# The opening's splits taken apart and sigmoid pairs set between the heavy ones in a hybrid backbone layer

## The chip, the cores and the metric

The kernel runs on one core of a Trainium2 chip. The metric is the device time of one execution in microseconds (us); lower is better. The engines have short names here as in the profile: PE is TensorE's matmuls and PEld its weight loads, DVE is VectorE, ACT is ScalarE, POOL is GpSimd, SP is the engine that issues most DMA transfers.

## What is computed

One layer with two token mixers side by side: a gated short convolution and an mLSTM that runs over the rows in both directions. Both read one wide input projection.

```python
hx = rmsnorm(x, g_norm) * (1 + scale) + shift          # 2048 x 1024
hc = rmsnorm(ctx, g_norm) * (1 + scale_c) + shift_c    # 256 x 1024
px = hx @ w_in + b_in                                  # 1024 x 11296
u = c_a * x_a
y_a = b_a * conv3(u) * silu(z_a)                       # conv along grid rows of 64
hn = headwise_rmsnorm(mlstm(q, k, v, gates)) * g_head
y_b = sigmoid(o) * hn * silu(z_b)
merged = sigmoid(g_a) * (y_a @ w_pa) + sigmoid(g_b) * (y_b @ w_pb)
out = rmsnorm(x + gate * (merged @ w_out + b_out), g_final)
```

`shift`, `scale` and `gate` come from `silu(c) @ w_ada + b_ada`. All of it is fp32.

## The kernel before

The 2048 rows are worked on in two halves of 1024. The big products keep fp32 accuracy by splitting each operand into a high part, rounded by a cast on ACT, and a low part, the remainder, which DVE gets by subtraction (`split`, L176 to L179); three matmuls, high by high, high by low and low by high, make one product. On top of that stands a scheme with seven block products in place of eight (Strassen and Winograd): a **pair** is a block of 256 output columns (two channel blocks, `i`) by two halves of 512 rows (`j`), and needs the seven left and seven right operands o = 0 to 6. The right ones are made once from the input (`xA`, slots `x`), the left ones from the weights as they stream in (`Stream`: raw weights `wr`, sums `sw`, high and low parts `wh` and `wl`). A pair is 7 x 4 x 3 = 84 matmuls of 128x512 (L415 in `pair`) into PSUM banks X, Y, W, Z, V. As products become ready, DVE adds them up (`u2` at L424, `u3` at L429, `added` at L914), and `fin` finishes the four blocks: one with the third product, the others with the fifth, sixth and seventh. The bank Z gets the seventh product on top of the fifth, so the sum at L914 of the block after the fifth has to be done before.

**The opening** (L1063 to L1241) makes `xA` and works out the first pair, q0, while inputs still land. For each of four column groups kk it has these steps: `ada` (L1092, four quarters n = 0 to 3, 8 matmuls each that the profile shows as 16 records) multiplies w_ada into PSUM tile `pu`, of which there is one; `modulation` (L1099 to L1101) takes shift and scale from there on DVE; `turn_to` (L212) transposes the normed rows on TensorE, four transposes to a block; `modulated` (L216 on ACT, L217 on DVE) applies shift and scale and gives blocks v11, v21, v12, v22; `cut_sums` makes four differences of them (L1136); `cut` splits seven parts; `mms` (L1110) are the matmuls of q0's first four products, `EARLY_OPS`, for this kk. TensorE's row is written out by hand; instructions in `pin` keep the order of the program on their engines, and nearly all of the opening on DVE and ACT is pinned.

**The first half's pairs** come in the order of the string `todo` (L1042). The letters are the column blocks of w_in: q, k, v; X, C, Z, B of the convolution branch; o and z (output gate and its silu gate); a and b (the merge gates g_a and g_b, whose `fin_s` is one tanh on ACT and a store). Of the `fin`s, C has most for DVE (a sum, a product and two shifted taps of the convolution, L982 to L989), z and Z two operations beside the sum, a, b and o none. After v3 the queue `later` runs beside the pairs, one step for each 4.3 matmuls (`run` with 0.235): `prep_b` (norms of the second half's rows, L205, their modulation, differences L295), `late_rows` (gate row L1357, rows of w_out times gate L1380), `ctx_scan` and `state_scan` (state updates: POOL weighs, L641, TensorE multiplies into the one bank `pn`, L646, DVE adds, L648 and L650). The order of the pairs is free as long as X comes before C, C before Z and B, Z before B, and o before z, as these hand tiles on.

Of the kernel before, what the change touches and what calls it, by code (L numbers as in the profile page):

```python
# [10 lines left out]
F32 = mybir.dt.float32  # L11
# [3 lines left out]
OP = mybir.AluOpType  # L15
# [26 lines left out]
def hybrid_kernel(ctx: ExitStack, tc, x, c, ctxt, c_ctx, w_ada, b_ada, g_norm, w_in, b_in,  # L42
                  w_conv, b_conv, g_head, w_pa, w_pb, w_out, b_out, g_final, out):
    nc = tc.nc
# [132 lines left out]
    def split(hi, lo, raw, eng=None, pinned=False):  # L177
        a = nc.scalar.copy(hi, raw)  # L178
        b = (eng or nc.vector).tensor_tensor(lo, raw, hi.bitcast(F32), op=OP.subtract)  # L179
# [123 lines left out]
    class Stream:  # L303
# [16 lines left out]
        def cut(self, raw):  # L320
            hi, lo = self.half()
            split(hi, lo, raw, None, self.pinned)
            return hi, lo

# [717 lines left out]
    todo = plan(kinds, "q0 q1 q2 q3 k0 v0 k1 v1 k2 v2 k3 v3 X0 C0 Z0 B0 X1 C1 Z1 B1 X2 C2 Z2 B2 X3 C3 Z3 B3 "  # L1042
                       "o0 z0 o1 z1 o2 z2 o3 z3 a0 a1 a2 a3 b0 b1 b2 b3")
# [82 lines left out]
    def cut(kk, o, v):
        if kk % 2 == 0:
            xA.claim((o,), (kk // 2,))
        split(xA.at(o, 0, kk), xA.at(o, 1, kk), v, None, True)

    def cut_first(kk):
        cut(kk, 0, vs[kk, 0])
        cut(kk, 2, vs[kk, 1])

    def less(d, a, b):
        pin(nc.vector.tensor_tensor(d, a, b, op=OP.subtract))  # L1136

    def cut_sums(kk):

        v11, v21, v12, v22 = (vs.pop((kk, n)) for n in range(4))  # L1140
        t1, t3 = uslot(), uslot()
        less(t1, v12, v11)
        less(t3, v22, v12)
        cut(kk, 4, t1)
        t2 = v11
        less(t2, v22, t1)
        cut(kk, 3, t3)

        def more():
            t4 = v21  # L1150
            less(t4, v21, t2)
            cut(kk, 1, t2)
            return (kk, 5, t4), (kk, 6, v22)
        return more

    def rest(todo):
        for a in todo:
            cut(*a)
# [17 lines left out]
    normed(4, 5)  # L1176
    modulated(0, (0, 1), None)
    cut_first(0)
    normed(5, 8)
    ada(1, (0,))  # L1180
    turn_to(0, (2, 3), (pa_, pd_))
    modulated(0, (2, 3))
    more = cut_sums(0)
    ada(1, (1,))
    turn_to(1, (0, 1), (pn_, pa_))
    ada(1, (2,))
    turn_to(1, (2, 3), (pa_, pd_))
    ada(1, (3,))
    rest(more())
    modulation(1)  # L1190
    modulated(1, range(4))
    cut_first(1)
    more = cut_sums(1)
    ada(2, (0, 1))
    turn_to(2, (0, 1), (pn_, pa_))
    ada(2, (2, 3))
    turn_to(2, (2, 3), (pa_, pd_))
    modulation(2)
    modulated(2, (0, 1))
# [452 lines left out]
```

## Time and profile before

| | us |
|---|---|
| median of 3 runs | 2679.39 (2679.29 to 2679.91) |
| profiled execution, device time | 2682.87 |
| its span, first to last instruction | 2681.2 |
| first half's pairs from X0 to B3, 383.4 to 714.4 us: TensorE busy / DVE busy | 319.8 / 271.5 |
| first half's pairs from o0 to b3, 714.4 to 1055 us: TensorE busy / DVE busy | 333.5 / 221.6 |

A row of the timeline holds start, duration, engine, line, operation, tiles (out<-in), shape, and in brackets the idle time ahead of it and what ended that. A row of the groups holds the count, then busy time and mean ns of one, then idle time ahead of them and what ended it. Buffer numbers are left out of the names: `x` stands for all slots of operands.

Where TensorE waits from 785 to 1055 us (in total, times, longest):

```profile
PE pn L646 <- DVE tk L650: 2.8, 2, 2.6
PE pn L646 <- DVE cst L648: 2.5, 2, 2.3
PE pn L646 <- POOL vw L641: 0.9, 1, 0.9
```

### The profile page before, as it was taken

The numbers are of one execution on the slowest core, as the hardware profiler recorded it, in microseconds if no ns is written. First come the engines' busy times: TensorE is split into PE (matmuls) and PEld (weight loads), VectorE is DVE, ScalarE is ACT, GpSimd is POOL, SyncE is SP. The second block draws the span as 40 slices with busy tenths as digits, with TensorE's granted clock in tenths as the row PEclk, the third lists the DMA queues.
The fourth block names the chain that finished last, engine by engine and source line by source line (L and its number), as shares of the span: only waits on it lengthen the run. The fifth ranks groups of instructions, "written<-read, shape, count | busy, mean of one in ns | idle before, by whom it ended". The sixth has DMA issues, their size and how long they took to land. (4 is left out here: it accounts for less than half of the span.)

```text
span 2681.2 us, 38175 instructions
## 1 busy us (share of the span) xinstructions
PE 2605.7 (97%) x12807; PEld 2172.1 (81%) x12807; DVE 1728.4 (64%) x3119; ACT 1098.8 (41%) x2269; POOL 1116.0 (42%) x1322
## 2 busy tenths in 40 slices
PE   7999999999999999999999999999999999999998
PEld 6788887887778887877887888888888888888777
DVE  5743238887976657477578667667766656554597
ACT  5433344333443335343443444344444544442333
POOL 1221223233345443235555565565655224422664
PEclk9999999999999999999999999999999999999999
DMA  8323353454643657425653654654466968868542
GB/s 229 96 93 108 102 150 119 157 181 138 228 141 101 179 171 241 127 86 151 193 159 117 198 169 127 181 164 138 151 194 192 307 213 268 256 200 275 200 162 95
DMA packets 373218, 452.99 MB, mean 169 GB/s; under 512 B 24429, under 2 KB 273949, under 8 KB 373021
## 3 DMA queue, kind: packets, MB, share of 16 engines
q1 hardware_dynamic: 372784, 450.46, 54.8%
q8 instruction: 102, 1.67, 0.3%
q14 instruction: 96, 0.78, 0.1%
q10 hardware_dynamic: 236, 0.08, 0.0%
HBM read 319.42 MB, written 131.03 MB: 168 GB/s over the span
## 5 line engine op out<-in xcount | busy, mean ns | idle before, releaser
L415 PE MATMUL pd<-x,wh 128*128 128x512 f32 x5320 | 1699.3, 398 | 22.1 <-DVE t2k L914 12.3
L415 PEld LDWEIGHTS pd<-x,wh 128*128 128x128 f32 x5320 | 986.9, 189 | 218.5 <-issue 25.2
L415 PE MATMUL pd<-x,wl 128*128 128x512 f32 x2660 | 1058.8, 398 | 0.0
L415 PEld LDWEIGHTS pd<-x,wl 128*128 128x128 f32 x2660 | 502.4, 189 | 99.3 <-issue 0.2
L178 ACT CAST wh<-sw 128x512 fp32r<-128x512 f32 x384 | 238.0, 620 | 513.7 <-PE pd L415 422.1
L179 DVE TENSOR_TENSOR wl<-sw,wh 128x512 fp32r<-128x512 f32 x384 | 311.9, 814 | 181.8 <-ACT wh L178 175.2
L178 ACT CAST wh<-wr 128x512 fp32r<-128x512 f32 x352 | 217.5, 618 | 372.1 <-PE pd L415 265.1
L348 POOL TENSOR_TENSOR sw<-wr,sw 128x512 f32<-128x512 f32 x95 | 135.6, 1427 | 446.1 <-DVE wl L179 389.8
L179 DVE TENSOR_TENSOR wl<-wr,wh 128x512 fp32r<-128x512 f32 x352 | 289.9, 824 | 37.9 <-ACT wh L178 36.8
L462 PE MATMUL pd<-x,wh 128*128 128x512 f32 x896 | 281.7, 396 | 0.0
L348 POOL TENSOR_TENSOR sw<-wr 128x512 f32<-128x512 f32 x95 | 130.0, 1369 | 239.6 <-DVE wl L179 233.7
L641 POOL TENSOR_SCALAR vw<-tk,wk 128x129 f32<-128x129 f32 x205 | 154.8, 759 | 125.8 <-PE pn L646 116.7
L462 PEld LDWEIGHTS pd<-x,wh 128*128 128x128 f32 x896 | 166.3, 188 | 32.0
L462 PE MATMUL pd<-x,wl 128*128 128x512 f32 x448 | 173.3, 397 | 0.0
L186 POOL TENSOR_SCALAR ssq<-ssq 128x1 f32<-128x1 f32 x128 | 37.3, 291 | 294.2 <-ACT hf L894 290.4
L914 DVE TENSOR_TENSOR t2k<-pd,u 128x512 f32<-128x512 f32 x168 | 115.5, 688 | 61.7 <-PE pd L415 60.6
L348 POOL TENSOR_TENSOR sw<-sw,wr 128x512 f32<-128x512 f32 x94 | 133.4, 1420 | 48.8 <-DVE wl L179 37.8
L892 ACT ACTIVATE hf<-pn,rd 128x128 f32<-128x128 f32 x128 | 47.0, 368 | 247.0 <-DVE rd L888 226.4
L348 POOL TENSOR_TENSOR sw<-wr,wr 128x512 f32<-128x512 f32 x94 | 132.9, 1414 | 18.7 <-DMA wr<-in_w_in_dram 9.4
L808 POOL TENSOR_SCALAR_AFFINE_SELECT mw<-mw 128x256 f32<-128x256 f32 x128 | 63.0, 512 | 120.9 <-DMA mw<-mwd 89.7
L879 PE MATMUL pn<-tk,pt 128*128 128x129 f32 x512 | 99.2, 276 | 4.7 <-DVE hb L893 4.7
L921 DVE SCALAR_TENSOR_TENSOR t2k<-pd,cols,u 128x512 f32<-128x512 f32 x73 | 54.8, 750 | 73.2 <-PE pd L415 68.3
(255 smaller groups left out, 3349.4 us busy)
## 6 DMA issues: line engine op xcount, KB each, us to landing
wr<-in_w_in_dram SPq DMA_DIRECT2D x176, 512.0 KB, 4.0
tk<-tokd SPq DMA_DIRECT2D x64, 386.0 KB, 3.7
mw<-mwd SPq DMA_DIRECT2D x44, 512.0 KB, 5.0
qkd<-t2k SPq DMA_DIRECT2D x64, 256.0 KB, 3.0
qk<-qkd SPq DMA_DIRECT2D x64, 256.0 KB, 4.0
tk<-tokd SPq DMA_DIRECT2D x48, 257.0 KB, 2.9
tokd<-t2k SPq DMA_DIRECT2D x32, 258.0 KB, 3.2
x<-in_w_ada_dram SPq DMA_DIRECT2D x16, 512.0 KB, 6.2
```

The source lines that it names most:

```text
L178: a = nc.scalar.copy(hi, raw)
L179: b = (eng or nc.vector).tensor_tensor(lo, raw, hi.bitcast(F32), op=OP.subtract)
L186: nc.gpsimd.tensor_scalar(dst, ss, 1.0 / n, EPS, op0=OP.mult, op1=OP.add)
L348: nc.gpsimd.tensor_tensor(s, a, b, op=op)
L415: nc.tensor.matmul(ps[b], op[wi][:, kk, :], xs.at(o, xi, kk), start=(fresh and kk + pi == 0), stop=(o == last[b] and kk == 3 and pi == 2), ...
L462: nc.tensor.matmul(pss[j], ops[k // 4][wi][:, k % 4, :], y(xi, k, j), start=(k + pi == 0), stop=(k == NK - 1 and pi == 2))
L641: pin(nc.gpsimd.tensor_scalar(vw, tk[:, VT], wk, None, op0=OP.mult))
L808: pin(nc.gpsimd.affine_select(mws[m][:, :, 0, d, :], mws[m][:, :, 0, d, :], pattern=[[0, 2], [s, P]], base=0, channel_multiplier=-s, compa ...
L879: nc.tensor.matmul(pn[:, d, :], pt[:, d, :], tk[:, VT], start=True, stop=False)
L892: nc.scalar.activation(hf, pn[:, 0, 0:P], AF.Copy, scale=rd[:, 0:1])
L914: nc.vector.tensor_tensor(t, ps, add, op=OP.add)
L921: nc.vector.scalar_tensor_tensor(dst, ps, bcol(col), add, op0=OP.add, op1=OP.add)
```

## The change

It has two parts. The order of the first half's pairs is another: o and z, and most of a and b, stand between the pairs of the convolution branch. And the opening is written in another order: `split` is taken apart into `high` (casts on ACT) and `low` (remainders on DVE), which are called apart; the four differences come in a row (`less`); the stream of weights holds its remainders back (`held`, `settle`); the last shift and scale (`ada(3)`, `modulation(3)`) comes ahead of the matmuls of q0; and the right operands 5 and 6 of the groups 2 and 3, which only the sixth and seventh product need, come after the first four products. What each engine computes in all is the same.

```diff
+            self.held = None
...
         def cut(self, raw):
             hi, lo = self.half()
-            split(hi, lo, raw, None, self.pinned)
+            if self.held is None:
+                split(hi, lo, raw, None, self.pinned)
+            else:
+                pin(nc.scalar.copy(hi, raw))
+                self.held.append((lo, raw, hi))
             return hi, lo
+
+        def settle(self):
+
+            for lo, raw, hi in self.held:
+                pin(nc.vector.tensor_tensor(lo, raw, hi.bitcast(F32), op=OP.subtract))
+            self.held = []
...
-    todo = plan(kinds, "q0 q1 q2 q3 k0 v0 k1 v1 k2 v2 k3 v3 X0 C0 Z0 B0 X1 C1 Z1 B1 X2 C2 Z2 B2 X3 C3 Z3 B3 "
-                       "o0 z0 o1 z1 o2 z2 o3 z3 a0 a1 a2 a3 b0 b1 b2 b3")
+    todo = plan(kinds, "q0 q1 q2 q3 k0 v0 k1 v1 k2 v2 k3 v3 X0 C0 a0 Z0 b0 B0 o0 z0 X1 C1 a1 Z1 b1 B1 o1 z1 "
+                       "X2 C2 a2 Z2 B2 o2 z2 X3 C3 a3 Z3 B3 o3 z3 b2 b3")
...
+    def high(kk, *parts):
+        for o, v in parts:
+            if kk % 2 == 0:
+                xA.claim((o,), (kk // 2,))
+            pin(nc.scalar.copy(xA.at(o, 0, kk), v))
+
+    def low(kk, *parts):
+        for o, v in parts:
+            pin(nc.vector.tensor_tensor(xA.at(o, 1, kk), v, xA.at(o, 0, kk).bitcast(F32), op=OP.subtract))
+
+    def blocks(kk):
+
+        return (0, vs[kk, 0]), (2, vs[kk, 1])
+
+    def less(kk):
 
         v11, v21, v12, v22 = (vs.pop((kk, n)) for n in range(4))
         t1, t3 = uslot(), uslot()
-        less(t1, v12, v11)
-        less(t3, v22, v12)
-        cut(kk, 4, t1)
-        t2 = v11
-        less(t2, v22, t1)
-        cut(kk, 3, t3)
...
+        for d, a, b in ((t1, v12, v11), (t3, v22, v12), (v11, v22, t1), (v21, v21, v11)):
+            pin(nc.vector.tensor_tensor(d, a, b, op=OP.subtract))
+        return (3, t3), (1, v11), (4, t1), (5, v21), (6, v22)
...
-    normed(4, 5)
+    normed(4, 6)
     modulated(0, (0, 1), None)
-    cut_first(0)
-    normed(5, 8)
-    ada(1, (0,))
+    normed(6, 8)
+    high(0, *blocks(0))
+    low(0, *blocks(0))
+    ada(1, (0, 1))
     turn_to(0, (2, 3), (pa_, pd_))
     modulated(0, (2, 3))
-    more = cut_sums(0)
-    ada(1, (1,))
+    ada(1, (2,))
     turn_to(1, (0, 1), (pn_, pa_))
-    ada(1, (2,))
+    parts = less(0)
+    high(0, *parts)
+    low(0, *parts[:2])
+    ada(1, (3,))
     turn_to(1, (2, 3), (pa_, pd_))
-    ada(1, (3,))
-    rest(more())
     modulation(1)
+    low(0, *parts[2:])
     modulated(1, range(4))
-    cut_first(1)
-    more = cut_sums(1)
     ada(2, (0, 1))
     turn_to(2, (0, 1), (pn_, pa_))
+    high(1, *blocks(1))
+    low(1, *blocks(1))
+    st.held = []
+    st.fill(2)
+    parts = less(1)
+    high(1, *parts)
     ada(2, (2, 3))
     turn_to(2, (2, 3), (pa_, pd_))
     modulation(2)
-    modulated(2, (0, 1))
-    rest(more())
-    modulated(2, (2, 3))
-    st.fill(2)
-    cut_first(2)
+    low(1, *parts)
+    modulated(2, range(4))
+    high(2, *blocks(2))
+    ada(3, (0, 1))
     turn_to(3, (0, 1), (pn_, pa_))
-    ada(3, (0,))
+    ada(3, (2,))
     turn_to(3, (2,), (pa_,))
-    ada(3, (1,))
+    ada(3, (3,))
+    st.settle()
     st.fill(4)
+    low(2, *blocks(2))
+    st.settle()
+    st.held = None
     ops.update((o, st.take(0)) for o in (0, 2, 1, 3))
     ps.update((b, dense_ps()) for _, b in EARLY_OPS)
-    mms(0, (0, 1))
-    more = cut_sums(2)
-    ada(3, (2, 3))
+    mms(0)
     modulation(3)
-    modulated(3, range(3))
-    mms(0, (2, 3))
+    modulated(3, (0, 1))
+    parts = less(2)
+    high(2, *parts[:2])
+    modulated(3, (2,))
     turn_to(3, (3,), (pn_,))
-    rest(more())
-    cut_first(3)
     modulated(3, (3,))
+    low(2, *parts[:2])
+    high(3, *blocks(3))
+    low(3, *blocks(3))
     mms(1)
     mms(2)
-    more = cut_sums(3)
-    rest(more())
+    high(2, parts[2])
+    low(2, parts[2])
+    late = less(3)
+    high(3, *late[:3])
+    low(3, *late[:3])
     mms(3)
     s1, u2, u3 = uslot(), uslot(), uslot()
-    nc.scalar.copy(s1, ps["X"])
+    pin(nc.scalar.copy(s1, ps["X"]))
     ops[4] = st.take(0)
-    fin(0, 0, ps["U"], s1)
+    for i in (3, 4):
+        for kk, part in ((2, parts[i]), (3, late[i])):
+            high(kk, part)
+            low(kk, part)
+        if i == 3:
+            fin(0, 0, ps["U"], s1)
     nc.vector.tensor_tensor(u2, ps["Y"], s1, op=OP.add)
     nc.vector.tensor_tensor(u3, ps["W"], u2, op=OP.add)
```

The first place to see is DVE around the last shift and scale of the opening (`gsc` and `shift` from `pu`). Before, remainders and differences of group 2 (`u`, `cv`, `t2k` and the operands `x`) stand ahead of it:

```order
L346 TENSOR_TENSOR sw_570<-wr_193 128x512
L179 TENSOR_TENSOR wl_573<-sw_570,wh_572 128x512
L1136 TENSOR_TENSOR u_586<-t2k_508,cv_497 128x512
L1136 TENSOR_TENSOR u_587<-t2k_510,t2k_508 128x512
L179 TENSOR_TENSOR x_120_591<-u_586,x_119_590 128x512
L1136 TENSOR_TENSOR cv_497<-t2k_510,u_586 128x512
L179 TENSOR_TENSOR x_122_596<-u_587,x_121_595 128x512
L1099 SCALAR_TENSOR_TENSOR gsc<-pu_538,cols_117 128x2x2
L1100 TENSOR_TENSOR shift<-pu_538,cols_117 128x2x2
L1101 TENSOR_TENSOR gsc<-gsc,cols_116 128x2x2
```

With the change it stands behind the weights' sums and remainders, and the four differences follow it in a row:

```order
L358 TENSOR_TENSOR sw_583<-wr_193 128x512
L1146 TENSOR_TENSOR x_98_519<-cv_510,x_97_518 128x512
L1146 TENSOR_TENSOR x_100_522<-cv_512,x_99_521 128x512
L334 TENSOR_TENSOR wl_581<-sw_578,wh_580 128x512
L334 TENSOR_TENSOR wl_586<-sw_583,wh_585 128x512
L1111 SCALAR_TENSOR_TENSOR gsc<-pu_524,cols_117 128x2x2
L1112 TENSOR_TENSOR shift<-pu_524,cols_117 128x2x2
L1113 TENSOR_TENSOR gsc<-gsc,cols_116 128x2x2
L1157 TENSOR_TENSOR u_615<-t2k_514,cv_510 128x512
L1157 TENSOR_TENSOR u_616<-t2k_516,t2k_514 128x512
L1157 TENSOR_TENSOR cv_510<-t2k_516,u_615 128x512
L1157 TENSOR_TENSOR cv_512<-cv_512,cv_510 128x512
```

Group 2's differences went from ahead of the last shift to behind it.

The second place is DVE at the end of the opening, from the remainder of the fifth product's weight (`wl` from `sw`, bank Z) to that of the sixth (`wl` from `wr`, bank V). Before:

```order
L921 SCALAR_TENSOR_TENSOR t2k_716<-pd_577,cols_116,u_706 128x512
L179 TENSOR_TENSOR x_130_641<-cv_620,x_129_640 128x512
L179 TENSOR_TENSOR x_132_645<-t2k_652,x_131_644 128x512
L179 TENSOR_TENSOR wl_713<-sw_562,wh_712 128x512
L1230 TENSOR_TENSOR u_707<-pd_579,u_706 128x512
L1231 TENSOR_TENSOR u_708<-pd_578,u_707 128x512
L179 TENSOR_TENSOR wl_722<-wr_195,wh_721 128x512
```

With the change:

```order
L179 TENSOR_TENSOR wl_701<-sw_576,wh_700 128x512
L1146 TENSOR_TENSOR x_139_705<-cv_512,x_138_704 128x512
L1146 TENSOR_TENSOR x_139_705<-cv_613,x_138_704 128x512
L933 SCALAR_TENSOR_TENSOR t2k_710<-pd_593,cols_116,u_694 128x512
L1146 TENSOR_TENSOR x_142_714<-t2k_516,x_141_713 128x512
L1146 TENSOR_TENSOR x_142_714<-t2k_634,x_141_713 128x512
L1248 TENSOR_TENSOR u_695<-pd_595,u_694 128x512
L1249 TENSOR_TENSOR u_696<-pd_594,u_695 128x512
L179 TENSOR_TENSOR wl_722<-wr_195,wh_721 128x512
```

The remainders of the operands 5 and 6 and the first block's end came between the two.

The third place is DVE in the eleventh pair of `later`'s stretch, which is Z2 before and a1 now, both behind a C pair. `acc` belongs to the gate row of `late_rows`, `u` are u2 and u3, the last row is the sum of the block after the fifth product. Before:

```order
L424 TENSOR_TENSOR u_5389<-pd_5373,u_5365 128x512
L179 TENSOR_TENSOR wl_5392<-wr_5194,wh_5391 128x512
L179 TENSOR_TENSOR wl_5416<-sw_5413,wh_5415 128x512
L1002 SCALAR_TENSOR_TENSOR t2k_5409<-t2k_5407,t2k_5409 128x512
L1357 SCALAR_TENSOR_TENSOR acc<-xb_5333,sc,acc 128x1024
L1003 TENSOR_TENSOR cv_5235<-cv_5235,t2k_5409 128x512
L429 TENSOR_TENSOR u_5435<-pd_5419,u_5389 128x512
L179 TENSOR_TENSOR wl_5438<-wr_5290,wh_5437 128x512
L914 TENSOR_TENSOR t2k_5454<-pd_5441,u_5435 128x512
```

With the change:

```order
L436 TENSOR_TENSOR u_5389<-pd_5373,u_5365 128x512
L179 TENSOR_TENSOR wl_5392<-wr_5194,wh_5391 128x512
L179 TENSOR_TENSOR wl_5413<-sw_5410,wh_5412 128x512
L1375 SCALAR_TENSOR_TENSOR acc<-xb_5333,sc,acc 128x1024
L441 TENSOR_TENSOR u_5432<-pd_5416,u_5389 128x512
L179 TENSOR_TENSOR wl_5435<-wr_5290,wh_5434 128x512
L926 TENSOR_TENSOR t2k_5451<-pd_5438,u_5432 128x512
```

Z's two operations are gone from between; the rest keeps its order. In the fourth pair (B0 before, Z0 now) the last of the four norms (L205) stands just ahead of such a sum, before and now.

More of the change, by code (lines that the diff above doesn't have):

```diff
@@ L1124, in modulated @@
             pin(modulate(v, pts.pop((kk, n)), kk + 4 * (n % 2), 0, eng))
[L1126 to L1138, printed above, removed]
+    def high(kk, *parts):
[9 more added lines that the diff above has]
+    def less(kk):
         v11, v21, v12, v22 = (vs.pop((kk, n)) for n in range(4))
         t1, t3 = uslot(), uslot()
-        less(t1, v12, v11)
-        less(t3, v22, v12)
-        cut(kk, 4, t1)
-        t2 = v11
-        less(t2, v22, t1)
-        cut(kk, 3, t3)
[L1149 to L1158, printed above, removed]
+        for d, a, b in ((t1, v12, v11), (t3, v22, v12), (v11, v22, t1), (v21, v21, v11)):
+            pin(nc.vector.tensor_tensor(d, a, b, op=OP.subtract))
+        return (3, t3), (1, v11), (4, t1), (5, v21), (6, v22)
     EARLY_OPS = ((0, "X"), (2, "U"), (3, "W"), (1, "Y"))
```

## The prediction

> **What bounds the kernel now.** I read the page first, then TensorE's timeline of the first 95 us, then who TensorE waited for in each stage.
>
> ```profile
> PE 2605.7 (97%) x12807; PEld 2172.1 (81%) x12807; DVE 1728.4 (64%) x3119; ACT 1098.8 (41%) x2269; POOL 1116.0 (42%) x1322
> ```
>
> TensorE is busy for 2605.7 of the span's 2681.2 us. The change leaves the matmuls as they are, so all it can win is the 75.5 us of TensorE's idle time and the stretches in which matmuls run at half the granted clock. Three pieces of the opening on TensorE (start, duration, idle before it and what ended that):
>
> ```profile
> 23.62 3.75 PE L1092 MATMUL pu<-sc,x 128*128 128x128 f32 x16 [2.86 <-DMA x<-in_w_ada_dram]
> ...
> 41.14 0.60 PE L212 MATMUL pt<-ident,xr 128*128 128x128 f32 x4
> ...
> 42.01 3.74 PE L1092 MATMUL pu<-sc,x 128*128 128x128 f32 x32
> 45.59 0.60 PE L212 MATMUL pa<-ident,xr 128*128 128x128 f32 x4
> ...
> 62.69 1.05 PE L212 MATMUL pt<-ident,xr 128*128 128x128 f32 x4 [3.13 <-ACT cv L216]
> ...
> 69.59 0.62 PE L1110 MATMUL pd<-x,wh 128*128 128x512 f32 x2
> ...
> 70.27 0.62 PE L1110 MATMUL pd<-x,wh 128*128 128x512 f32 x2
> ...
> 76.01 0.50 PE L1110 MATMUL pd<-x,wl 128*128 128x512 f32 x1 [1.27 <-DVE wl L179]
> ...
> 85.49 0.62 PE L415 MATMUL pd<-x,wh 128*128 128x512 f32 x2
> ```
>
> The opening ends at 85.49, where the first L415 matmul of the ordinary pairs starts. Two waits stand out, 3.13 and 1.27 us. VectorE in the stretch between the third shift and scale and the last weight remainder shows why:
>
> ```profile
> 45.78 0.16 DVE L1099 SCALAR_TENSOR_TENSOR gsc<-pu,cols 128x4 f32<-128x4 f32 x1 [0.37 <-PE pu L1092]
> ...
> 61.41 0.16 DVE L1099 SCALAR_TENSOR_TENSOR gsc<-pu,cols 128x4 f32<-128x4 f32 x1
> ...
> 82.29 0.69 DVE L179 TENSOR_TENSOR wl<-sw,wh 128x512 fp32r<-128x512 f32 x1 [0.74 <-ACT wh L178]
> ```
>
> ```profile
> L179 DVE TENSOR_TENSOR x<-cv,x 128x512 fp32r<-128x512 f32 x10 | 6.5, 686 | 5.0 <-ACT x L178 5.0
> ...
> L179 DVE TENSOR_TENSOR wl<-sw,wh 128x512 fp32r<-128x512 f32 x4 | 2.8, 691 | 2.1 <-ACT wh L178 2.1
> L921 DVE SCALAR_TENSOR_TENSOR t2k<-pd,cols,u 128x512 f32<-128x512 f32 x3 | 2.2, 748 | 2.3 <-PE pd L1110 2.3
> ...
> L179 DVE TENSOR_TENSOR wl<-wr,wh 128x512 fp32r<-128x512 f32 x3 | 2.0, 686 | 1.0 <-ACT wh L178 1.0
> ```
>
> The second fence groups VectorE's work from 45 to 83 us (busy, mean ns, idle before). 5.0 + 2.1 + 2.3 + 1.0 = 10.4 us of these 38 are waits, mostly because each remainder (lo) is queued straight behind the ScalarE cast (hi) it needs. The last shift and scale (61.41) stands in that row, so TensorE got its last transposes late.
>
> In the first half's heavy pairs TensorE's waits end mostly on VectorE's sums (t2k):
>
> ```profile
> 465.25 0.90 PE L415 MATMUL pd<-x,wh 128*128 128x512 f32 x2 [2.04 <-DVE t2k L914]
> ...
> 529.84 0.70 PE L415 MATMUL pd<-x,wh 128*128 128x512 f32 x2 [1.76 <-DVE t2k L914]
> ...
> 609.38 1.19 PE L415 MATMUL pd<-x,wh 128*128 128x512 f32 x2 [2.73 <-DVE t2k L914]
> ...
> 692.54 0.70 PE L415 MATMUL pd<-x,wh 128*128 128x512 f32 x2 [3.53 <-DVE t2k L914]
> ```
>
> By the sequence of pairs these lie in B0, Z1, Z2 and Z3. The clock stands in the windows view (us; busy of PE, PEld, DVE, ACT, POOL; granted clock; DMA share, GB/s):
>
> ```profile
> 62.80:66.20 3.40, 3.40 (x11) 2.83 (x12) 1.69 (x3) 3.40 (x7) 0.00 (x0) 0.50 0.02 5
> 76.50:79.90 3.40, 3.40 (x10) 2.62 (x9) 1.35 (x3) 0.00 (x0) 0.00 (x0) 0.50 0.00 0
> 608.90:612.30 3.40, 2.92 (x7) 2.38 (x8) 3.40 (x6) 1.99 (x4) 0.00 (x0) 0.51 0.52 154
> 530.40:533.80 3.40, 3.40 (x17) 2.81 (x16) 3.05 (x6) 2.49 (x5) 0.00 (x0) 1.00 0.83 254
> 694.20:697.70 3.50, 3.50 (x17) 2.87 (x16) 3.50 (x6) 2.08 (x4) 0.00 (x0) 1.00 0.81 267
> ```
>
> About 3.4 us at 0.50 follow the waits of 3.13, 1.27 and 2.73 us, none follow those of 1.76 and 3.53. One such stretch costs 1.7 us of TensorE work, where it comes.
>
> **The opening, step by step.** Distances from row to row: two groups of four transposes 0.87 (41.14 to 42.01); one quarter of the shift and scale (16 records) 3.58 / 2 = 1.79 (42.01 to 45.59); three matmuls 0.68 (69.59 to 70.27). Twelve of these are 2.72. A VectorE operation of 512 columns lasts 0.686 and the next starts after about 0.60, as its end is overlapped. On ScalarE:
>
> ```profile
> 38.95 0.78 ACT L216 ACTIVATE t2k<-pa,shift,gsc 128x512 f32<-128x512 f32 x1
> 39.62 0.78 ACT L216 ACTIVATE t2k<-pd,shift,gsc 128x512 f32<-128x512 f32 x1
> ...
> 50.47 1.14 ACT L178 CAST wh<-wr 128x512 fp32r<-128x512 f32 x2
> 51.50 1.15 ACT L178 CAST x<-cv 128x512 fp32r<-128x512 f32 x2
> ```
>
> so 0.67 from one modulation to the next and 0.52 from cast to cast. I laid the new order of the three engines along these distances:
>
> - Up to 23.62 nothing moves on TensorE, since that row waits for a load. The two quarters ahead of the transposes run at half speed as now, to about 29.6; all rows are normed by 25.7.
> - From there TensorE has six double transposes (5.2), ten quarters (17.9), two single transposes (0.9) and seven times twelve matmuls (19.1): 43.1 us, which would end at 72.7.
> - The second shift and scale is 0.87 + 1.79 + 0.87 + 1.79 behind 29.6, the third 8.9 and the fourth 9.3 behind the one before; with some 0.2 for the way to VectorE they fall at 35.2, 44.1 and 53.6 (45.78 and 61.41 now for the last two). The last loads are issued by 42.25 and need about 6.2, so they land by 48.5, ahead of the 51.6 at which TensorE wants them.
>
> ```profile
> 34.73 7.52 SPq L1061 DMA_DIRECT2D x<-in_w_ada_dram x4
> x<-in_w_ada_dram SPq DMA_DIRECT2D x16, 512.0 KB, 6.2
> ```
>
> - VectorE from 44.1: 42 operations at 0.60 and 0.8 for the small ones, 26 us, and 1.9 us of waits that are left (for the last shift, the casts and sw): its last weight remainder starts at 72.2 (82.29 now).
> - One wait is added. Between the remainders of the fifth and the sixth weight (wl of Z and V) stand seven operations, two now; counted the same way the sixth ends at 70.2, and TensorE wants it at 68.0. Behind it in TensorE's row wait the rest of V, the seventh product and q1, so its 2.3 us count in full (with 0.1 for Z's remainder 2.4).
>
> The first L415 matmul comes at 72.7 + 2.4 = 75.1, with 0.2 for the ways between engines at 75.3: **10.2 us earlier**. VectorE gives the same: 82.29 - 72.2 = 10.1. The ScalarE and VectorE operations are the same in number, so nothing is added. The differences in a row cost nothing by themselves, as VectorE is waiting for the third shift (42.6 to 44.1) when they are done. If the 2.3 us wait were followed by a half-speed stretch, 1.7 would come back: 8.5. From below I take 7 (VectorE 10% slower in its 28 us), from above 11.5 (10.4 of waits and the rest of the clock).
>
> **The pairs.** Per pair the later work (norms, differences, rows of w_out, states) is drawn by the number of matmuls, so it stays at its place and the pairs are exchanged under it. Their weight loads and stores go with them, the same in number; the DMA shares of 0.52 to 0.83 above leave them room. At Z1's place stands o0 behind B0, at Z3's place o1 behind B1: the conv work of C, which runs over into the next pair, is gone from there, so 1.76 and 3.53 go. At Z2's place stands a1, but still behind a C. VectorE there:
>
> ```profile
> 603.92 0.68 DVE L1002 SCALAR_TENSOR_TENSOR t2k<-t2k,t2k 128x512 f32<-128x512 f32 x1
> ...
> 606.75 0.68 DVE L1003 TENSOR_TENSOR cv<-cv,t2k 128x512 f32<-128x512 f32 x1
> ...
> 608.55 0.68 DVE L914 TENSOR_TENSOR t2k<-pd,u 128x512 f32<-128x512 f32 x1
> ```
>
> Only the first two leave the row ahead of the sum that TensorE waits for: 2 x 0.60 = 1.2 of the 2.73, and 1.5 stays. That is less than the 1.76 which no slow stretch followed, so I take its 1.7 too (0 if not). The 2.04 us at B0's place stays: the sum waits behind a norm,
>
> ```profile
> 463.14 0.75 DVE L205 TENSOR_SCALAR xb<-xb,rs 128x1024 f32<-128x1024 f32 x1 [1.87 <-POOL rs L187]
> ```
>
> which the new row keeps ahead of the sum. Z0's short waits,
>
> ```profile
> PE pa L1323 <- DVE t2k L217: 1.1, 2, 0.9
> ```
>
> in all 1.1, give 0.5. C2 with a2 now lies beside differences like those that Z1 had: 1.76 - 1.2, +0.5. C3, Z3, B3 now lie beside the state updates, through one PSUM bank (pn):
>
> ```profile
> L646 PE MATMUL pn<-vw,tk 128*128 128x129 f32 x192 | 38.0, 279 | 7.1 <-DVE cst L648 3.2 <-DVE tk L650 2.8 <-POOL vw L641 0.9
> PE pn L646 <- DVE tm L650: 1.4, 3, 0.6
> PE pn L646 <- DVE tk L650: 1.2, 2, 0.7
> ```
>
> Beside o, z, a, b these 192 records waited 7.1 us (first row, 714 to 1055 us); in the second half, where X C Z B lie beside the same updates, the waits for VectorE are 2.6 us in 720 us (the other two). So I add 1.5, between 0 and 7.1. Sum: -1.76 - 3.53 - 1.2 - 1.7 - 0.5 + 0.5 + 1.5 = **-6.7 us**, from -15 (all four waits and both slow stretches gone) to 0.
>
> Nothing else is edited, and the stages behind keep their rows. The profiled execution took 2682.87 us (span and 1.7 around it), 3.5 above the median 2679.39. The terms are differences, so they go onto the median: 2679.4 - 10.2 - 6.7 = **2662.5**.
>
> On the clock, the Trainium skill ("TensorE: Matmul & The Clock Gate", section "Why this matters for your kernels") says to leave no idle gap over some 3 us between bursts, or the clock falls to half. This trace differs: 2.73 was followed by 0.51, 3.53 by 1.00. By that rule the 1.7 at Z2's place would not be won: 2664.2.
>
> **Rivals.**
> - *The opening alone pays* (0.17): C's overrun goes into a as it went into Z, and the states take back what o0 and o1 give: 2679.4 - 10.2 = 2669. For it: the same conv rows stand ahead of a1's sum. Against it: Z1's and Z3's places have no C ahead.
> - *All waits on sums go* (0.14): VectorE catches up in every light pair and the norm no longer binds: -15 in place of -6.7: 2654.
> - *The opening doesn't do what it says* (0.07): its loads or VectorE's row, busy for 26 of 28 us, set the same end, and the pairs alone pay: 2673.
> - *Slower* (0.06): the state updates. There are 96 (two records each), where they are dense one to two or three steps of the later queue, a step to 4.3 matmuls of 0.23, or about 2.5 us. Each needs VectorE to empty pn, and in C each of the last three blocks brings four operations, 2.7 us with their 0.686, to the remainders that are there anyway, within the 2.72 of twelve matmuls. From the point where VectorE is over 2.5 us behind, every update stalls TensorE, with slow stretches behind it. Some 70 of the 96 updates at 0.35 us are 24 us: 2679.4 - 16.9 + 24 = 2686. Against it stand the 2.6 us above.
>
> **How the numbers follow.** My forecast has 0.56, with 2657 to 2668 as its own range. 2654 to 2671 takes in the first two rivals and leaves out some 0.2. A measurement of this kernel tells apart about 0.2% (5.4 us): faster than 2674 are the forecast, the first two rivals and half of the third, 0.90; within it 0.05; slower 0.05.
>
> **What would show it.** First L415 matmul at 75 (73 to 78), last shift and scale on VectorE near 53.6, TensorE without a wait from 30 to 67 us, then one of about 2 us for wl. No wait for t2k near 515 and 675 (Z1's and Z3's old places, moved), one of 1 to 2 us in a1, one of 2 us with the norms of the first group behind a0. Waits of L646 below 9 us up to the half's end. I would be wrong if VectorE's row in the opening has waits of over 4 us after 44, or if L646's waits double.

## The result and the profile after

The changed kernel took **2661.77 us** (median of four runs) against 2679.34 before: ratio 0.9935, 95% interval 0.9924 to 0.9947, 17.6 us faster. A later set of five runs gave 2661.48 (0.9934, 0.9921 to 0.9948). Its profiled execution took 2660.47 us with a span of 2658.7; the one before had 2682.87 and 2681.2. The profiled pair is thus 22.4 us apart, more than the medians, and the difference has to be explained too.

First line of the changed kernel's page (busy us, share of the span, instructions):

```profile
PE 2594.5 (98%) x12807; PEld 2166.7 (81%) x12807; DVE 1722.6 (65%) x3119; ACT 1099.0 (41%) x2269; POOL 1123.8 (42%) x1322
```

TensorE (PE) has the same 12807 matmuls. It is busy for 11.2 us less. Fewer stretches at half speed explain at most 6.6 us of that (they cost 22.3 us of the profile before and 15.7 of this one); what the rest is stays open.

The opening's end on TensorE in the changed kernel (start, duration, idle before it and what ended that), then the last shift and scale and the last weight remainders on VectorE (DVE):

```profile
68.11 0.61 PE L1122 MATMUL pd<-x,wh 128*128 128x512 f32 x2
70.70 0.50 PE L1122 MATMUL pd<-x,wl 128*128 128x512 f32 x1 [1.97 <-DVE wl L179]
...
75.85 0.62 PE L427 MATMUL pd<-x,wh 128*128 128x512 f32 x2
```

```profile
54.00 0.16 DVE L1111 SCALAR_TENSOR_TENSOR gsc<-pu,cols 128x4 f32<-128x4 f32 x1 [0.42 <-PE pu L1104]
...
69.97 0.68 DVE L179 TENSOR_TENSOR wl<-wr,wh 128x512 fp32r<-128x512 f32 x1
...
72.65 0.69 DVE L179 TENSOR_TENSOR wl<-sw,wh 128x512 fp32r<-128x512 f32 x1 [0.74 <-ACT wh L178]
```

The first ordinary matmul (L427, L415 before) stands at 75.85 (85.49 before), the last shift and scale at 54.00 (61.41 before). The one wait that is left behind 30 us is that for the sixth weight's remainder, 1.97 us.

TensorE's main waits in the 32 pairs of the first half, changed kernel:

```profile
456.10 0.54 PE L427 MATMUL pd<-x,wh 128*128 128x512 f32 x1 [2.65 <-DVE t2k L926]
596.35 0.47 PE L427 MATMUL pd<-x,wh 128*128 128x512 f32 x1 [1.03 <-DVE t2k L926]
751.72 0.47 PE L427 MATMUL pd<-x,wh 128*128 128x512 f32 x1 [0.96 <-DVE t2k L926]
783.02 0.35 PE L658 MATMUL pn<-vw,tk 128*128 128x129 f32 x1 [2.33 <-DVE cst L660]
888.17 0.35 PE L658 MATMUL pn<-vw,tk 128*128 128x129 f32 x1 [0.95 <-DVE tk L662]
895.14 0.35 PE L658 MATMUL pn<-vw,tk 128*128 128x129 f32 x1 [1.46 <-DVE tk L662]
1033.10 0.45 PE L658 MATMUL pn<-vw,tk 128*128 128x129 f32 x1 [2.96 <-DVE tk L662]
```

The waits of 1.76 and 3.53 us at Z1 and Z3 have no successor. That of 2.73 became 1.03 in a1; that behind the norms (2.04 in B0) stands in Z0 as 2.65. New are 0.96 in a2, behind C2, and 0.95 and 1.46 in a3, behind C3; the last two stand at matmuls of the state updates (L658, L646 before). The 2.33 and 2.96 were there before, as 2.31 and 2.60.

The same windows view for both kernels: the opening, the pairs q, k and v, the 16 pairs from X0, the next 16, and all behind (us; busy of PE, PEld, DVE, ACT, POOL; granted clock; DMA share, GB/s). Changed kernel, then the one before:

```profile
0.00:75.85 75.85, 62.13 (x408) 56.57 (x408) 49.31 (x94) 40.66 (x69) 11.94 (x28) 0.93 0.77 220
75.85:373.60 297.75, 295.51 (x1582) 249.10 (x1580) 116.54 (x213) 112.33 (x217) 64.59 (x76) 1.00 0.34 105
373.60:696.20 322.60, 317.75 (x1419) 260.52 (x1418) 239.75 (x314) 133.45 (x226) 106.32 (x88) 0.99 0.55 179
696.20:1042.30 346.10, 335.09 (x1538) 275.04 (x1537) 250.54 (x411) 132.70 (x204) 166.53 (x160) 0.99 0.51 153
1042.30:2658.70 1616.40, 1584.03 (x7867) 1325.45 (x7865) 1066.43 (x2089) 679.88 (x1554) 774.40 (x970) 1.00 0.58 182
```

```profile
0.00:85.49 85.49, 67.21 (x408) 58.62 (x408) 50.18 (x94) 41.07 (x69) 10.99 (x28) 0.92 0.68 195
...
383.40:714.40 331.00, 319.80 (x1419) 261.36 (x1418) 271.49 (x349) 124.25 (x214) 107.81 (x88) 0.99 0.52 165
714.40:1055.00 340.60, 333.51 (x1537) 274.04 (x1536) 221.61 (x375) 138.87 (x214) 156.22 (x160) 0.99 0.54 164
1055.00:2681.20 1626.20, 1589.49 (x7867) 1329.03 (x7866) 1068.40 (x2090) 682.41 (x1556) 776.35 (x970) 0.99 0.59 181
```

By stage: opening -9.6, first 16 pairs -8.4, next 16 pairs **+5.5**, and **-9.8** in the stages behind, whose code is the same. Of the 5.5 the forecast had 2.0, of the -9.8 nothing. The experiments ask whether the -9.8 belongs to the change, what gives the 5.5 back, and which part of the opening pays.

### The profile page after: what moved, and what is told of

Its sections match the earlier page's. It is cut to its first block, busy times and chain, and to the rows that moved or that the text cites. A ratio compares the mean times of both kernels' runs of the same rounds, so it can differ in the third digit from the quotient of the medians.

```text
span 2658.7 us, 38177 instructions
## 1 busy us (share of the span) xinstructions
PE 2594.5 (98%) x12807; PEld 2166.7 (81%) x12807; DVE 1722.6 (65%) x3119; ACT 1099.0 (41%) x2269; POOL 1123.8 (42%) x1322
## 4 chain that ended last, share of the span: by engine, by line
PE 48%; DVE 3%; DMA 2%; issue 1%; POOL 1%; ACT 0%; SPq 0%; DVEq 0%; POOLq 0%; ACTq 0%
PE pd L427 29%; PE pd L474 11%; PE pn L891 2%; PE pn L892 2%; PE pa L834 1%; PE pu L658 1%; DMA mgd<-t2k 1%; DVE wl L179 1%; PE pa L849 1%; PE pn L658 0%; PE pa L669 0%; DVE xt L1596 0%; DVE xt L1605 0%; DMA x<-wod 0%; DVE cv L999 0%
## 5 line engine op out<-in xcount | busy, mean ns | idle before, releaser
L427 PE MATMUL pd<-x,wh 128*128 128x512 f32 x5320 | 1695.9, 397 | 15.9 <-DVE xt L1605 8.5
L427 PEld LDWEIGHTS pd<-x,wh 128*128 128x128 f32 x5320 | 985.1, 189 | 209.9 <-issue 19.4
L427 PE MATMUL pd<-x,wl 128*128 128x512 f32 x2660 | 1057.3, 397 | 0.0
L427 PEld LDWEIGHTS pd<-x,wl 128*128 128x128 f32 x2660 | 501.8, 189 | 99.3 <-issue 0.2
L179 DVE TENSOR_TENSOR wl<-sw,wh 128x512 fp32r<-128x512 f32 x382 | 303.2, 795 | 182.0 <-ACT wh L178 177.1
L653 POOL TENSOR_SCALAR vw<-tk,wk 128x129 f32<-128x129 f32 x205 | 161.9, 794 | 120.2 <-PE pn L658 109.7
L891 PEld LDWEIGHTS pn<-tk,pt 128*128 128x128 f32 x512 | 86.8, 190 | 16.2 <-issue 5.8
```

The lines of the kernel that those rows point to most:

```text
L427: nc.tensor.matmul(ps[b], op[wi][:, kk, :], xs.at(o, xi, kk), start=(fresh and kk + pi == 0), stop=(o == last[b] and kk == 3 and pi == 2), ...
L653: pin(nc.gpsimd.tensor_scalar(vw, tk[:, VT], wk, None, op0=OP.mult))
L891: nc.tensor.matmul(pn[:, d, :], pt[:, d, :], tk[:, VT], start=True, stop=False)
```

## What the clock records show, and how lengths are compared

Half-speed stretches make two executions of one kernel differ, so they are dealt with first. In the 14 profiles of this case (the two above and twelve below) every half-speed stretch begins a whole number of steps of 3.413 us after every other of the same execution, to 0.02 us: a raster that runs by itself. Two waits of the kernel before, in windows laid on this raster (same columns):

```profile
605.50:608.91 3.41, 1.14 (x6) 0.60 (x4) 3.41 (x5) 0.00 (x0) 0.24 (x1) 1.00 0.26 92
608.91:612.33 3.42, 2.95 (x7) 2.40 (x8) 3.42 (x6) 2.02 (x4) 0.00 (x0) 0.50 0.52 153
687.44:690.85 3.41, 1.57 (x7) 0.95 (x6) 3.41 (x5) 0.00 (x0) 0.33 (x1) 1.00 1.02 378
690.85:694.27 3.42, 1.73 (x8) 1.45 (x9) 3.07 (x5) 1.81 (x3) 0.00 (x0) 1.00 0.83 255
694.27:697.68 3.41, 3.41 (x17) 2.81 (x16) 3.41 (x6) 2.01 (x4) 0.00 (x0) 1.00 0.80 264
```

The wait of 2.73 us falls into one step, which keeps 1.14 us of TensorE work, and the next step runs at 0.50. The longer wait of 3.53 us is cut by a boundary into two steps with 1.57 and 1.73 us of work, and no step is slow. That is why 2.73 cost a slow stretch and 3.53 none, which the prediction could only note. Over the steps between 90 and 2480 us of all 14 profiles that are not slow themselves: with 1.0 to 1.8 us of idle time 113 steps, none followed by a slow one; with 1.8 to 1.94 us 3 of 10; with 1.95 us or more 33 of 33. Outside these bounds (from 10 us on) idle time alone does not decide: of 35 steps with 1.0 to 1.8 us three were followed by a slow one, with 1.49, 1.70 and 1.76 us. The first of them holds the wait of 1.27 us in the opening of the kernel before:

```profile
73.00:76.50 3.50, 2.01 (x7) 1.13 (x8) 3.50 (x6) 1.33 (x3) 0.00 (x0) 0.99 0.22 75
```

What else counts there stays open. The Trainium skill ("TensorE: Matmul & The Clock Gate", "Why this matters for your kernels") puts the limit at gaps of some 3 us; here a wait of 2.04 was followed by a slow step, and the measurement decides.

So a stage's length at full speed is its length less half of its half-speed time, and a run's is its span times its mean granted clock. Both are used below; the rest of the span is the clock's loss. This is an estimate: a slow step in which TensorE also waits costs less than half of its length, and the runs' granted clocks are on record to 0.001, which is up to 1.3 us of one run. In the four sets of runs that the kernel before has beside the experiments, on three chips, its mean at full speed is 2654.5 to 2654.8 us, so runs of different sets are compared at full speed.

## Experiments

**The two halves of the change by themselves, and the change again** (one chip, five runs each).

The opening alone, the sequence of pairs as before:

```diff
-"... X0 C0 a0 Z0 b0 B0 o0 z0 X1 C1 a1 Z1 b1 B1 o1 z1 X2 C2 a2 Z2 B2 o2 z2 X3 C3 a3 Z3 B3 o3 z3 b2 b3"
+"... X0 C0 Z0 B0 X1 C1 Z1 B1 X2 C2 Z2 B2 X3 C3 Z3 B3 o0 z0 o1 z1 o2 z2 o3 z3 a0 a1 a2 a3 b0 b1 b2 b3"
```

> The opening of the change with the old sequence of pairs. Theory (two independent gains, the opening's about -9.6 us and the pairs' about -3 in their stage): the first L427 matmul at 75.8, the pairs' stage as before shifted by -9.6, median about 2669.5 us against 2679 before. Rival (the -9.8 us that the changed kernel won in stages behind the pairs belongs to the opening, by another phase of everything behind it): -18 to -20 us, about 2660. Rival (that -9.8 is luck of single executions): -9.6 with later stages within 2 us of the old ones.

The pairs alone: the kernel before with the upper one of these two strings.

> The old opening with the new sequence of pairs. Theory: the old opening's end (85.5) stays; the first 16 pairs win about 8 us, the last 16 give back about 5, in all -3 in the stage: about 2676 us. Rival (the gain of -9.8 behind the stage belongs to the sequence of pairs, since it moves what the later queue holds when the stage ends): -11 to -14, about 2666. Rival (order of pairs is worth the predicted -6.7 and the run seen was unlucky): about 2672.5.

The changed kernel, unedited:

> The changed kernel once more, to be compared with its parts on one chip. If the parts add: its gain is the sum of those of the opening alone and the pairs alone within 2 us, about -17.5. If the gain behind the stage needs both or is chance, the sum of the two differs from it by over 3 us, or its later stages differ between the two profiles by over 3 us.

| kernel | median us | ratio, interval | at full speed, mean us | lost to the clock, mean us |
|---|---|---|---|---|
| before (9 runs) | 2678.24 | | 2654.6 | 22.0 |
| opening alone | 2666.13 | 0.9954, 0.9941 to 0.9966 | 2648.2 | 16.0 |
| pairs alone | 2667.91 | 0.9962, 0.9949 to 0.9974 | 2650.9 | 15.5 |
| both | 2661.48 | 0.9934, 0.9921 to 0.9948 | 2644.3 | 14.9 |

At full speed the parts add: -6.4 and -3.7 against -10.3 together. What the clock takes does not add: -6.0 and -6.5 against -7.1, each with a standard error of 1.2 to 1.8 us. By the medians each part alone gave more than its theory (-12.1 for -9.6, -10.3 for -3), and the pairs came nearer to their rival; but what is over is clock, not work. The gap is 5.4 us with a standard error of 2.1; why the clock's share does not add stays open.

**The kernel before once more**, unedited, for a second profile.

> The kernel before once more, for a second profile. Theory (TensorE's idle stretches belong to the order of the work and come back; what varies from run to run is where the half-speed stretches fall, since they start on a raster of 3.413 us that runs by itself, after a raster step in which TensorE was idle for over about 1.95 us): the waits of 2.04, 2.73, 3.53, 2.31, 2.60, 2.59 us (near 465, 609, 692, 800, 1047, 1068) within 0.7 us of these, all half-speed starts a multiple of 3.413 us apart, other waits followed by them than in the first profile. Rival (the waits of 2.59 near 1068 and 1.64 near 1994, gone in the changed kernel, are chance): they are missing here too.

One run, 2674.17 us, span 2672.5. The waits at Z1, Z2, Z3 came back as 1.76, 2.78 and 3.53. Those of 2.31 and 2.60 were 2.31 and 3.15, the one behind the norms 1.64 in place of 2.04. The stages behind the half, and the wait near 1068, in this second profile (windows, timeline) and in the first (timeline):

```profile
1056.10:2672.50 1616.40, 1584.80 (x7868) 1325.78 (x7866) 1070.65 (x2089) 679.82 (x1554) 775.65 (x970) 1.00 0.58 182
```

```profile
1068.08 0.33 PE L657 MATMUL pa<-ident,t2k 128*128 128x128 f32 x1 [1.26 <-ACT t2k L919]
```

```profile
1068.50 0.33 PE L657 MATMUL pa<-ident,t2k 128*128 128x128 f32 x1 [2.59 <-ACT t2k L919]
```

The kernel before did these stages in 1616.40 us as well, as long as the changed kernel took. The wait near 1068 was half as long, that near 1994 missing, and the half-speed time there 9.8 in place of 20.8 us. So the rival held: **the -9.8 us is the bad luck of one profiled execution**, not a gain of the change.

**The sixth weight's remainder ahead of the operands'**, in the changed kernel:

```diff
     ops[4] = st.take(0)
+    st.fill(1)
     for i in (3, 4):
...
-    st.fill(1)
     for n, (o, b) in enumerate(((4, "Z"), (5, "V"), (6, "Z"))):
```

> The changed kernel with the sixth weight (V) cast and its remainder taken ahead of the remainders of operands 5 and 6, no work added. Theory (VectorE is the bound of the opening's end, its last remainder at 72.65 being fixed by its 26 us of work): the 1.97 us wait for V's wl goes, a wait of about the same size for the operands of the seventh product or for its weight takes its place, first L427 matmul at 75.0 to 75.9: gain 0 to 0.8 us. Rival (the order alone cost the 2.0): first L427 matmul at 73.9, gain 2.0 us.

The opening's end on TensorE:

```profile
71.87 0.73 PE L1122 MATMUL pd<-x,wh 128*128 128x512 f32 x2 [1.64 <-ACT wh L178]
...
75.00 0.61 PE L427 MATMUL pd<-x,wh 128*128 128x512 f32 x2
```

As the theory had it: the wait of 1.97 is gone, one of 1.64 for the seventh weight stands in its place. At full speed the opening ends at 71.6 (75.00 less half of 6.8), as in the unedited repeat (71.8). The median, 2658.31 us (0.9931, 0.9917 to 0.9944), lies 3.2 under the repeat's, with 2644.2 us at full speed against 2644.3: the work takes the same. Their means are only 1.2 us apart, of which 1.1 is clock. The forecast's 2.3 us wait was not a cost of where V stands; as the same time at full speed shows, it is what is left of a bound by VectorE's row and the casts that feed it.

**High and low together again**, in the changed kernel:

```diff
     def high(kk, *parts):
...
-            pin(nc.scalar.copy(xA.at(o, 0, kk), v))
+            split(xA.at(o, 0, kk), xA.at(o, 1, kk), v, None, True)
     def low(kk, *parts):
-        for o, v in parts:
-            pin(nc.vector.tensor_tensor(xA.at(o, 1, kk), v, xA.at(o, 0, kk).bitcast(F32), op=OP.subtract))
+        pass
...
-    st.held = []
...
-    st.settle()
...
```

> The changed kernel with each remainder (lo) straight behind its cast (hi) again, all else kept. The opening's end less half of its half-speed time is 71.7 us in the changed kernel, 78.6 in the one before. Theory (apart was needed to win VectorE's waits for casts, 5.0 + 2.1 + 1.0 us in the old opening, of which some half comes back): 74 to 76 by that count, 2 to 4 us slower. Rival (the order of the transposes and shifts wins it all): within 0.7 of 71.7.

2667.65 us (0.9966, 0.9952 to 0.998), 6 us above the changed kernel. By the means it is 7.1 us, 3.2 of them at full speed (2647.6 against 2644.3) and the rest clock. VectorE's groups from 45 us to the opening's end (busy, mean ns, idle before): first this kernel, then the changed one.

```profile
L179 DVE TENSOR_TENSOR x<-cv,x 128x512 fp32r<-128x512 f32 x10 | 6.6, 686 | 4.1 <-ACT x L178 4.1
...
L179 DVE TENSOR_TENSOR wl<-sw,wh 128x512 fp32r<-128x512 f32 x4 | 2.8, 690 | 2.1 <-ACT wh L178 2.1
```

```profile
L1146 DVE TENSOR_TENSOR x<-cv,x 128x512 fp32r<-128x512 f32 x10 | 6.6, 685 | 0.7 <-ACT x L1142 0.7
...
L179 DVE TENSOR_TENSOR wl<-sw,wh 128x512 fp32r<-128x512 f32 x2 | 1.4, 688 | 0.7 <-ACT wh L178 0.7
...
L334 DVE TENSOR_TENSOR wl<-sw,wh 128x512 fp32r<-128x512 f32 x2 | 1.3, 685 | 0.0
```

The waits for casts are back, 6.2 us against 1.4 (two of the four remainders `wl` from `sw` stand at L334 in the changed kernel). The opening ends at 81.40 with 13.7 us at half speed, 74.6 at full speed: 3 us later, as expected. With the remainders back beside their casts, the last shift and scale came to VectorE at 58.01 in place of 54.00. Taking the remainders apart from their casts, with what this lets come earlier, brings some 3 of the opening's 7 us at full speed. What brings the other 4 no run separates.

**The last half of the fourth shift and scale back behind two products**:

```diff
-    ada(3, (2,))
     turn_to(3, (2,), (pa_,))
-    ada(3, (3,))
...
-    mms(0)
-    modulation(3)
-    modulated(3, (0, 1))
+    mms(0, (0, 1))
     parts = less(2)
     high(2, *parts[:2])
+    ada(3, (2, 3))
+    modulation(3)
+    modulated(3, (0, 1))
+    mms(0, (2, 3))
```

> The changed kernel with the last half of the fourth shift and scale back behind the first two operands' products, as it stood before, and the differences of the third block pair ahead of it. Theory (the last transposes and all that follows on VectorE wait for this shift: some 3.6 us of TensorE work and 24 matmuls of order): the opening's end less half of its half-speed time 73.5 to 75, against 71.7: 2 to 3 us slower. Rival (VectorE has enough else to do up to then): within 0.7 of 71.7.

2660.35 us (0.9936, 0.9922 to 0.9949), 72.1 at full speed: the rival held. The shift came to VectorE at 54.86, 0.9 later than in the changed kernel's first profile. That profile ran one more step at half speed ahead of it; in the repeat, which has as many as this run, the shift stands at 53.34, so the delay is 1.5 us, the length of the six matmuls (two products) put ahead. Its place on TensorE is worth some 1 us at most here. The edit does not put VectorE's row back, though. In the kernel before, TensorE was done with this shift at 57.36,

```profile
53.63 3.73 PE L1092 MATMUL pu<-sc,x 128*128 128x128 f32 x32
```

and VectorE took it only at 61.41, behind remainders and differences. What that order cost by itself no run shows.

**The norms in two steps**, the multiplication one step of the later queue behind:

```diff
...
-                norm(xt[i], nc.vector)
+                rss.append(stats(xt[i]))
+                if i:
+                    nc.vector.tensor_scalar(xt[i - 1], xt[i - 1], rss[i - 1], None, op0=OP.mult)
...
```

`stats` is the norm without its last multiplication on VectorE.

> The changed kernel with the norms of the second half's rows in two steps: sums of squares first, VectorE's multiplication one step of the later queue later, so that the VectorE row no longer waits for POOL's rs. Nothing is left out. Theory: the wait of 1.3 to 2.65 us for t2k in Z0 (near 455) falls below 0.5, and with it the chance of a half-speed stretch there: 1.5 to 4 us off, about 2658.5. Rival (the sum is late for VectorE's own work, the norm only stands in front of it): the wait stays above 1 us, no gain.

2660.43 us (0.9936, 0.9924 to 0.9949), the wait in Z0 1.95 us. The edit did not do what it says: written later in the program, the multiplication still stood where it had stood in VectorE's row. The run shows what it waits for. POOL, then VectorE:

```profile
451.57 1.68 POOL L370 TENSOR_TENSOR sw<-wr 128x512 f32<-128x512 f32 x1 [2.07 <-DVE wl L179]
453.20 0.65 POOL L215 TENSOR_TENSOR rs<-ss 128x1 f32<-128x1 f32 x1
```

```profile
454.80 0.75 DVE L1351 TENSOR_SCALAR xb<-xb,rs 128x1024 f32<-128x1024 f32 x1 [1.00 <-POOL rs L187]
```

POOL has the sum of squares behind a weight sum, which itself waited 2.07 us for VectorE, and VectorE then waits for POOL. Pinned further back, the multiplication was tried once more below.

**C3 five pairs earlier**, the 20th of the 32 in place of the 25th, where the state updates begin. The changed opening with `X C a Z b B` four times, then `o0 z0 ... o3 z3`:

> The changed opening with a third sequence of pairs: X C a Z b B four times, then the eight pairs o and z; C3 so comes six places ahead of where the change has it, before the state updates are dense. Theory (what the changed kernel gives back in its last 16 pairs, 11.0 us of idle time against 6.9, comes from C3's overrun beside the state updates): the waits of L658 near 888 and 895 (0.95 + 1.46) and those in B3, b2 go, the first 18 pairs keep about 5 us of idle time: 2 to 4 us faster than the changed kernel. Rival (any light or heavy pair beside the updates waits as much): idle time of the 32 pairs stays at 15 to 16 us, no gain.

2671.26 us (0.9978, 0.9968 to 0.9988): some 10 us slower than the changed kernel, though the theory held in its stage. What the L658 matmuls (L646 before) waited for, in the 16 pairs from the end of the first 16 on: the kernel before, the changed one, this one (us, times):

```profile
  DVE cst L648: 3.2, 3
  DVE tk L650: 2.8, 2
  POOL vw L641: 0.9, 1
```

```profile
  DVE tk L662: 6.2, 4
  DVE cst L660: 3.1, 2
  issue: 0.8, 1
```

```profile
  DVE tk L662: 3.3, 3
  DVE cst L660: 2.0, 4
  POOL vw L653: 1.4, 1
```

6.9, 10.1 and 6.7 us; the stage at full speed took 338.9, 342.7 and 339.4. What the changed kernel gives back is mostly the waits of the state updates beside C3 and behind it; 0.96 us is the wait in a2, which now lies among the first 16 pairs as 1.73. But at the start of the second half stands

```profile
1051.20 0.79 PE L427 MATMUL pd<-x,wl 128*128 128x512 f32 x1 [14.52 <-DVE wl L179]
```

VectorE has z3's four outputs and the wide remainders of the second half's operands ahead of the new weights. With b2 and b3 last, these remainders lie beside pairs that leave VectorE nothing.

**The three edits together** (V first, norms in two steps, this sequence):

> The changed kernel with three edits: V's remainder first, the norms in two steps, and the sequence X C a Z b B four times. If they add: 0.5 + 2 to 3 + 2 to 4 us faster than the changed kernel, about 2655 (2652 to 2658). If one of them only moves a wait: 2658 to 2661.

2669.98 us (0.9971, 0.996 to 0.9983). It has the same wait, 12.63 us; neither expectation knew of it.

**C3 early and b2 b3 last**: `X0 C0 a0 Z0 b0 B0 X1 C1 a1 Z1 b1 B1 X2 C2 a2 Z2 B2 X3 C3 a3 Z3 B3 o0 z0 ... o3 z3 b2 b3`.

> The changed opening with the sequence X C a Z b B, X C a Z b B, X C a Z B, X C a Z B, then the pairs o and z four times, then b2 b3: C3 six places earlier as in the run e9_front, but the two pairs b, which leave VectorE nothing, last again. Theory (the wait of 14.52 us at the start of the second half in e9_front came from the wide remainders that stand on VectorE ahead of the new half's weights, beside z3's work; without that the early C3 wins what the changed kernel gives back): the last 16 pairs at 339 to 340 us at full speed (342.5 in the changed kernel), the first 16 within 1 us of its 320.5, no wait over 3 us behind: 2657 to 2659. Rival (b2 and b3 earlier were not the cause of the 14.52): that wait comes back, 2668 to 2672.

2657.48 us (0.9933, 0.9917 to 0.9948). The long wait is gone; the last 16 pairs take 340.4 us at full speed, the first 16 take 321.2. Over its five runs it has 2643.4 at full speed against 2644.3 for the repeat of the changed kernel and 2642.5 for that kernel's first four runs, so the 2.3 us won in the last 16 pairs do not show in the whole. The lower median is clock (12.8 lost against 14.9 and 16.0), and this kernel is not settled as faster.

**The norms' multiplications held back and pinned there**, in that kernel:

```diff
...
+            yield from gap(4)
+            for i in range(4):
+                pin(nc.vector.tensor_scalar(xt[i], xt[i], rss[i], None, op0=OP.mult))
+                yield
...
```

> As e11_c3early, and the norms' multiplications on VectorE held back until all four sums of squares have been issued and kept at that place in VectorE's row (in e6_norm they stood at their old places, though written later). Theory (VectorE's row waits there for POOL's rs, which stands on POOL behind a weight sum that waits for VectorE): the wait for t2k in Z0 (1.3 to 2.65) falls below 0.7, idle time of the first 16 pairs 1 to 2 us less than in e11_c3early, 1 to 3 us faster. Rival (the transposes of these rows then wait instead): a wait of over 1 us on xb in their place, no gain.

2660.18 us (0.9935, 0.9921 to 0.9949): no gain, as the rival had it. The wait for t2k in Z0 (1.94 us in the kernel it is built on) is gone, and the transposes wait in its place, twice under 1 us where the rival had one wait of over 1:

```profile
400.97 0.33 PE L1355 MATMUL pa<-ident,xb 128*128 128x128 f32 x1 [0.81 <-DVE xb L1350]
```

```profile
458.77 0.33 PE L1355 MATMUL pa<-ident,xb 128*128 128x128 f32 x1 [0.94 <-DVE xb L1350]
```

## Why the prediction was right, and where it was not

The forecast of 2662.5 us is 0.7 above the median. That it is so near is in part luck. The 16.9 us that it took off were 11.8 of work and waits and 5.1 of half-speed stretches (3.4 in the opening, 1.7 at Z2's place); between the means of the first experiments' runs lie 10.3 and 7.1. Means over the profiles with the same opening, or the same sequence of pairs (three of the old opening, seven of the new; three of the old sequence, six or seven of the new), in us:

| stage | full speed, old | new | half-speed loss, old | new | sum | forecast |
|---|---|---|---|---|---|---|
| opening | 78.4 | 71.1 | 6.8 | 4.4 | -9.7 | -10.2 |
| 16 pairs from X0 | 327.5 | 320.2 | 2.3 | 0.3 | -9.3 | -8.7 |
| next 16 pairs | 339.1 | 342.7 | 2.3 | 2.7 | +4.0 | +2.0 |
| behind | 1613.8 | 1612.1 | 7.1 | 6.5 | -2.3 | 0 |

The last row is not a gain that these runs establish: single profiles there range from 1611.3 to 1615.7 us at full speed with the old sequence and from 1610.9 to 1614.2 with the new.

- **The opening** (-10.2): right in size and place, and in the part of the mechanism that was tested. First L427 at 75.85 (forecast 75.3), last shift at 54.00 (53.6), V's remainder done at 70.65 (70.2), the wait 1.97 (2.3), VectorE's waits from 45 us on 0.7 + 0.7 + 0.4 + 0.1 = 1.9 (1.9). Three sums of the prediction are 0.1 to 0.2 us too high: 44.1 + 9.3 gives 53.4 and not 53.6, 44.1 + 26 + 1.9 gives 72.0 and not 72.2, 70.2 - 68.0 gives 2.2 and not 2.3. Waits for casts pay, as the run with high and low together shows. That the last shift and scale ahead pays by its place on TensorE was not confirmed: put back, the opening's 72.1 us at full speed compare with 70.7 to 71.8 in the kernels that have it ahead.
- **Z1, Z3, Z2's place**: 1.76 and 3.53 went whole; 2.73 became 1.03, where 1.5 was to stay, and no slow stretch followed. The wait behind the norms stayed, as forecast, at 1.3 to 2.65 us. The short L1323 waits (L1341 now) did not shrink by 0.5: 0.89 against 0.86 in the largest.
- **C2 with a2** (+0.5): the wait there is 0.96 us.
- **The state updates** (+1.5): **mis-sized, by 1.7 us**. Their waits rose by 3.2, from 6.9 to 10.1, past the 9 us that the prediction had named as its limit. The term was taken from the second half, where X C Z B beside "the same updates" showed 2.6 us. They are not as dense there: 218 matmul records in the 723 us from 1237 to 1960, against 192 in 266 us in the first half (781.4 to 1047.6). The early-C3 kernels bring the waits back to 6.7 and 8.5; these move other pairs too, so that C3 alone is the cause is argued, not shown.
- **Nothing moves behind**: held, though the profiled pair showed -9.8. Putting the terms onto the median and not onto the one profile was right: that execution was 3.5 us above its median.
- **The clock**: one stretch was counted for Z2 and the opening's two were in the 10.2; the runs lost 22.0 us to it before and 14.9 after. With the raster it is not a wait's length alone that decides whether a slow stretch follows: one of 2.73 us leaves 1.95 in a single step for (1.46 + 0.78) / 3.41 = 0.66 of the positions, one of 3.53 us for 0.89, if all positions are alike. By this estimate Z2 and Z3 were worth 1.55 x 1.7 = 2.6 us of clock between them, not 1.7 and 0. The three profiles of the old sequence had one, none and two slow steps there, 3 where the estimate gives 4.7: too few to tell.

## What to carry to other kernels

Count a wait on TensorE twice: by its length, and by the chance that a step of the clock's raster keeps too little work; here one of 1.7 us cost its length, one of 2.7 us its length and in two of three profiles another 1.7. Before a late piece of work is moved next to light pairs, find out how dense the other queues are there (the state updates beside C3) and what the light pairs at the end cover (the wide remainders beside b2 and b3). And take a second profile of the unchanged kernel before a gain in code that wasn't touched is explained: here 9.8 us of it were one execution's luck.

## What the runs showed of the hardware that was not expected

The granted clock changes in steps of 3.413 us on a raster that has no fixed place against the program. Between 90 and 2480 us 33 of 33 steps with at least 1.95 us of TensorE idle time were followed by a step at 0.50, none of 113 with 1.0 to 1.8 us; outside these bounds 3 of 35 of the latter were. A wait of the changed kernel, the one behind the norms, shows the same (windows; the step with the wait and the one behind it):

```profile
453.00:456.40 3.40, 0.75 (x4) 0.33 (x3) 2.40 (x4) 0.41 (x1) 1.40 (x4) 0.99 0.46 140
456.40:459.80 3.40, 3.40 (x9) 2.63 (x8) 2.45 (x5) 2.48 (x5) 0.00 (x0) 0.50 0.07 22
```

In the repeat the same wait was 1.32 us and no slow step followed.
